# The first norm of a two-layer encoder: a scaled input turned by transposes, in place of a product with a diagonal

## The chip, the core and the metric

The kernel runs on one core of one Trainium2 chip. The metric is the time of one execution on the device, in microseconds; lower is better. The engines are TensorE (PE, with its weight loads as PEld), VectorE (DVE), ScalarE (ACT), GpSimd (POOL) and SyncE (SP), which here only issues loads and stores.

## What is computed

Two layers of a streaming encoder on 256 tokens of 1024 channels, in float32. Cut to what matters here:

```python
for l in range(DEPTH):                       # DEPTH = 2
    h = rmsnorm(x, pre_norm_g[l])            # x * rsqrt(mean(x*x) + EPS) * g, along the channels
    proj = h @ w_in[l]                       # 1024 -> 10432
    (u, v, z_a, c_q, c_kv, k_rope, z_b, x_c, z_c, g_a, g_b, g_c) = split(proj)
    y_a = gmlp_spatial(u, v, ...) * silu(z_a)
    y_b = mla_attention(c_q, c_kv, k_rope, ...) * silu(z_b)
    y_c = rg_lru(x_c, ...) * silu(z_c)
    merged = sigmoid(g_a) * (y_a @ w_proj_a[l]) + sigmoid(g_b) * (y_b @ w_proj_b[l]) + sigmoid(g_c) * (y_c @ w_proj_c[l])
    x = x + rmsnorm(merged @ w_out[l], post_norm_g[l])
```

The change touches how the first layer's `h` is made, and what stands around it.

## The kernel before, in words

The 256 tokens are two tiles of 128 (`NT = 2`), the 1024 channels eight tiles of 128 (`KT = 8`). The weights are streamed in chunks, 1 MB for most of them. A chunk is loaded by SyncE's queue into one of three raw buffers (`load`, L186), and is then split into two tiles of the type float32r: a high part (ScalarE, L242) and the remainder (VectorE, L243). A product is three passes of TensorE: high by high, high by low, low by high (L280 to L283, L407 to L409, L521 to L523). Three pairs of split tiles exist (`pairs`); `done` gives one back and `pump` splits the next chunk into it, and then asks for further loads, of which each waits until its raw buffer has been split.

The order of the work on each engine is the order in which the program writes it (`tc.manual_schedule()`, L432); nothing is reordered. A wait therefore holds all that was written behind it on the same engine, and a load that waits holds SyncE's queue.

The head of the program (L433 to L503) goes as follows. GpSimd writes `ones`, `mhalf` and the identity. ScalarE's queue loads the eight rows of `pre_norm_g` (`g8`). SyncE's queue loads token tile 0 in two halves (L439), the first half of chunk 0, token tile 1 (L440), the second half of chunk 0, chunks 1 and 2, four tables of the rotary embedding (L443 to L446) and nine small rows of constants (`layer_consts`, L297 to L307), which TensorE turns later in one transpose (L319) before the last of the eight rank steps.

Fourteen products of `ones` (`warm`, L453) fill TensorE while the input arrives. For a token tile, `first_norm` (L457) squares one half on ScalarE and the other on VectorE and makes the factor `rstd` (a sum on VectorE, L372, a power on GpSimd, L373). `diagonal` (L465) puts the factor on a diagonal, and `first_turn` (L470) multiplies the eight channel tiles by it (L473), which scales and transposes in one product; the result is evicted tile by tile, 128 columns each, by ScalarE with the gain as its scale (`hT[0]`, L477), and by VectorE, which leaves the remainder (`hT[1]`, L479). The gain as a column, `g0`, comes from a transpose of `g8` (L488, L489). `second_norm` (L492) runs between the two halves of the split of chunk 0: it makes tile 1's factor and then evicts tile 0. `second_turn` (L501) turns tile 1; it is called from within the first rank step, behind its first two rows of tiles, and it also splits chunks 1 and 2.

The rank steps (`ranks`, L513) multiply the four first chunks, each of 4 x 128 rows and 384 or 320 columns: chunk 0 by tiles 0 and 1, chunk 1 by both, and so on; chunks 0 and 2 need the channel tiles 0 to 3 of `hT`, chunks 1 and 3 the tiles 4 to 7. After them comes the first of the wide products (`recur_in`, L658, through L281 to L283).

The second layer's norm is made otherwise: `pre_norm` (L380) squares on ScalarE, scales 512 columns at a time on VectorE with the gain as a row (L388), and `pre_transpose` (L391) turns them by transposes (L396) and evicts 512 columns at a time (L399, L400).

Of the kernel before, what the change touches and what calls it, by code (L numbers as in the profile page):

```python
# [13 lines left out]
P = 128  # L14
# [3 lines left out]
NT = 2  # L18
# [67 lines left out]
def tile_trunk(ctx: ExitStack, tc, I, out):  # L86
# [99 lines left out]
    def load(c, parts=1, mid=None):  # L186
        n = c.kt * c.cols
        c.raw = raw_()
        if c.lru is None:
            raw, src, m = v2(c.raw[:, :n], c.cols), c.src(), c.kt // parts  # L190
            for i in range(parts):
                nc.sync.dma_start(raw[:, i * m : (i + 1) * m], src[:, i * m : (i + 1) * m])
                if i == 0 and mid:
                    mid()
            return
# [101 lines left out]
    def layer_consts(l, rows):  # L297
        G.memset(rows[64:R_N], 0.0)
        for name, r0, n in (
# [3 lines left out]
            nc.sync.dma_start(rows[r0 : r0 + n], I[name][l].rearrange("(t p) -> t p", p=P))  # L303
        nc.sync.dma_start(rows[R_CW : R_CW + 40], I["lru_conv_w"][l].rearrange("w (t p) -> (w t) p", p=P))
        for name, r0 in (("lru_b_a", R_BA), ("lru_b_x", R_BX)):
            nc.sync.dma_start(rows[r0 : r0 + NB, :BW], I[name][l].rearrange("(b p) -> b p", p=BW))
# [125 lines left out]
    with tc.manual_schedule():  # L432
# [7 lines left out]
        load(chunks[0], parts=2, mid=lambda: nc.sync.dma_start(X[:, 1], I["x"][0, P : 2 * P, :]))  # L440
        state["dma"] = 1
        loads_to(2)
        nc.sync.dma_start(cosT, I["cosT"])  # L443
        nc.sync.dma_start(sinT, I["sinT"])
        nc.sync.dma_start(cosK, I["cosK"].rearrange("(t p) f -> p t f", p=P))
        nc.sync.dma_start(sinK, I["sinK"].rearrange("(t p) f -> p t f", p=P))  # L446

        lc = layer_consts(0, slot("rows", (P,)))


        def warm(n):
            for _ in range(n):
                mm(aux()[:, :P], ones, ones, start=True, stop=True)  # L453

        g0 = small("g0", KT)

        def first_norm(t):  # L457

            ss = sums(2)
            mean_square(X[:, t, :512], ss[:, 0:1])  # L460
            x = X[:, t, 512:]
            V.scalar_tensor_tensor(tmp(), x, 1.0 / D, x, ALU.mult, ALU.mult, accum_out=ss[:, 1:2])
            return rsqrt_sum(ss)

        def diagonal(r):  # L465
            d = tmp()[:, :P]
            V.tensor_scalar(d, ident, r, None, ALU.mult)
            return d

        def first_turn(t, d, take, mid=None):  # L470
            ps = [take(), take()]
            for k in range(KT):
                mm(ps[k // 4][:, k % 4 * P : (k % 4 + 1) * P], X[:, t, k * P : (k + 1) * P], d, start=True, stop=True)  # L473
            for b in range(2):
                todo = [(b * 4 + k, ps[b][:, k * P : (k + 1) * P]) for k in range(4)]
                for k, o in todo:
                    act(hT[0][:, t, k], o, AF.Copy, scale=g0[:, k : k + 1])  # L477
                for k, o in todo:
                    V.scalar_tensor_tensor(  # L479
                        hT[1][:, t, k], o, g0[:, k : k + 1], f(hT[0][:, t, k]), ALU.mult, ALU.subtract  # L480
                    )
                if b == 0 and mid:
                    mid()

        warm(14)
        d0 = diagonal(first_norm(0))
        ps = aux()
        nc.tensor.transpose(ps[:, :KT], g8, ident[:KT, :KT])  # L488
        V.tensor_copy(g0, ps[:, :KT])  # L489
        ds = []  # L490

        def second_norm():  # L492
            r = first_norm(1)
            first_turn(0, d0, bank, lambda: ds.append(diagonal(r)))
            warm(1)

        split(chunks[0], parts=2, mid=second_norm)
        state["split"] = 1
        loads_to(3)

        def second_turn():  # L501
            first_turn(1, ds[0], aux, lambda: pump(1, parts=2))
            pump(parts=2)  # L503

        for l in range(L):
# [53 lines left out]
            for i in range(8):  # L559
                j, t = (i // NT, i % NT) if l == 0 else (i % 4, i // 4)  # L560
                if i == 7:
                    layer_consts2(lc)
                ranks(j, t, turns.get((j, t)))
# [533 lines left out]
```

## Time and profile before

| | |
|---|---|
| time of the runs shown, three | 788.27, 788.53, 789.82 us; median 788.53 |
| the profiled execution, its own time | 790.08 us |
| its span, from the first to the last instruction | 788.3 us |
| mean granted TensorE clock over the span | 0.997 |
| loaded and stored by DMA | 163.43 MB, 207 GB/s on average |

The page gives each engine's busy time, the span in 40 slices, the DMA queues, the chain of work that ended last, and the costliest groups of instructions. Of one instruction the timeline gives the start from the start of the span and the length, both in us, then the engine, the line, the operation and the tiles, `out<-in`, and in brackets how long its engine stood idle ahead of it and who released it. A line of the windows has the busy time of PE, PEld, DVE, ACT and POOL in one stretch, the number of instructions behind each, the clock that was granted to TensorE (1.00 is full speed), the busy share of the DMA engines, and what they moved in GB/s. A product of two plain float32 tiles shows as two records in the count of a row.

### The profile page before, as it was taken

Reading aid. Unit: us, or ns where it says so; the run is one execution under the profiler, and the core shown is the slowest. Engines: PE = TensorE matmul, PEld = TensorE weight load, DVE = VectorE, ACT = ScalarE, POOL = GpSimd, SP = SyncE. Lnnn points to the kernel's source line nnn. Section 1 sums busy time; section 2 is a strip of 40 time slices with the busy share of each in tenths; the row PEclk is TensorE's granted clock in tenths of the full one; section 3 lists DMA queues with packets and bytes.
Section 4 is the critical chain, followed back from the end, with each engine's and each line's share of the span. In section 5 each row is a group of like instructions: output and inputs, shape, how many; then the busy total and the mean of one; then the engine's idle time right before and its main releaser. Section 6 shows DMA issues by size and latency. Waiting matters only on the chain.

```text
span 788.3 us, 15228 instructions
## 1 busy us (share of the span) xinstructions
PE 778.4 (99%) x6381; PEld 771.4 (98%) x6381; DVE 540.4 (69%) x708; ACT 472.3 (60%) x705; POOL 39.2 (5%) x78
## 2 busy tenths in 40 slices
PE   8999999999999999999999999999999999999996
PEld 8999999999999999999999999999999999999996
DVE  5587776676569579556666887767665776885562
ACT  5687675446595585433556868544657856744441
POOL 1100420000000000000010006000000000000000
PEclk9999999999999999999999999999999999999999
DMA  7845657469989767556357555764799869566521
GB/s 226 284 151 190 210 178 212 130 169 305 295 235 293 244 195 262 187 187 215 114 173 241 167 181 167 241 162 130 215 315 289 255 223 317 181 219 213 180 88 54
DMA packets 162669, 163.43 MB, mean 207 GB/s; under 512 B 16510, under 2 KB 159272, under 8 KB 162600
## 3 DMA queue, kind: packets, MB, share of 16 engines
q1 hardware_dynamic: 162584, 162.45, 66.5%
q8 instruction: 50, 0.82, 0.4%
q14 instruction: 19, 0.16, 0.0%
q10 hardware_dynamic: 16, 0.00, 0.0%
HBM read 150.91 MB, written 11.53 MB: 206 GB/s over the span
## 4 chain that ended last, share of the span: by engine, by line
PE 96%; issue 2%; DMA 1%; ACT 1%; DVE 0%; SPq 0%; POOLq 0%; POOL 0%; DVEq 0%; ACTq 0%
PE mm L281 24%; PE mm L282 24%; PE mm L283 24%; PE mm L409 2%; PE mm L407 2%; PE mm L408 2%; PE mm L715 1%; PE mm L523 1%; PE mm L521 1%; PE mm L522 1%; PE aux L829 1%; PE aux L756 1%; DMA X<-in_x_dram 1%; PE mm L907 1%; PE mm L906 1%
## 5 line engine op out<-in xcount | busy, mean ns | idle before, releaser
L243 DVE TENSOR_TENSOR wlo<-raw,whi 128x2048 fp32r<-128x2048 f32 (+5 forms) x123 | 263.9, 2149 | 135.1 <-ACT whi L242 134.8
L281 PE MATMUL mm<-hT,whi 128*128 128x256 f32 x1088 | 306.8, 282 | 0.0
L283 PE MATMUL mm<-hT,wlo 128*128 128x256 f32 x1088 | 304.9, 280 | 0.0
L282 PE MATMUL mm<-hT,whi 128*128 128x256 f32 x1088 | 304.9, 280 | 0.0
L242 ACT ACTIVATE whi<-raw 128x2048 fp32r<-128x2048 f32 (+5 forms) x123 | 221.0, 1802 | 90.4 <-PE mm L282 71.2
L282 PEld LDWEIGHTS mm<-hT,whi 128*128 128x128 f32 x1088 | 204.9, 188 | 0.5 <-issue 0.5
L281 PEld LDWEIGHTS mm<-hT,whi 128*128 128x128 f32 x1088 | 204.9, 188 | 0.5 <-issue 0.5
L283 PEld LDWEIGHTS mm<-hT,wlo 128*128 128x128 f32 x1088 | 204.8, 188 | 0.0
L281 PE MATMUL mm<-ya,whi 128*128 128x256 f32 x128 | 36.1, 282 | 1.0 <-ACT t L861 1.0
L407 PE MATMUL mm<-whi,hT 128*128 128x256 f32 x128 | 36.5, 285 | 0.0
L409 PE MATMUL mm<-whi,hT 128*128 128x256 f32 x128 | 36.1, 282 | 0.0
L282 PE MATMUL mm<-ya,whi 128*128 128x256 f32 x128 | 36.0, 281 | 0.0
L283 PE MATMUL mm<-ya,wlo 128*128 128x256 f32 x128 | 36.0, 281 | 0.0
L281 PE MATMUL mm<-yc,whi 128*128 128x256 f32 x128 | 36.0, 281 | 0.0
L408 PE MATMUL mm<-wlo,hT 128*128 128x256 f32 x128 | 36.0, 281 | 0.0
L281 PE MATMUL mm<-yb,whi 128*128 128x256 f32 x128 | 35.9, 281 | 0.0
L283 PE MATMUL mm<-yb,wlo 128*128 128x256 f32 x128 | 35.9, 281 | 0.0
L282 PE MATMUL mm<-yc,whi 128*128 128x256 f32 x128 | 35.9, 281 | 0.0
L283 PE MATMUL mm<-yc,wlo 128*128 128x256 f32 x128 | 35.9, 280 | 0.0
L282 PE MATMUL mm<-yb,whi 128*128 128x256 f32 x128 | 35.9, 280 | 0.0
L373 POOL TENSOR_TENSOR rstd<-rstd,mhalf 128x1 f32<-128x1 f32 x8 | 4.4, 549 | 547.7 <-DVE rstd L372 547.7
L428 ACT ACTIVATE mg<-acc 128x512 fp32r<-128x512 f32 x8 | 5.1, 632 | 42.8 <-DVE acc L881 42.8
(253 smaller groups left out, 1601.8 us busy)
## 6 DMA issues: line engine op xcount, KB each, us to landing
raw<-in_w_in_dram SPq DMA_DIRECT2D x76, 1024.0 KB
raw<-in_w_proj_a_dram SPq DMA_DIRECT2D x8, 1024.0 KB
raw<-in_w_proj_b_dram SPq DMA_DIRECT2D x8, 1024.0 KB
raw<-in_w_proj_c_dram SPq DMA_DIRECT2D x8, 1024.0 KB
raw<-in_w_out_dram SPq DMA_DIRECT2D x8, 1024.0 KB
xs<-xh SPq DMA_DIRECT2D x16, 320.0 KB
raw<-in_mla_w_uq_dram SPq DMA_DIRECT2D x8, 576.0 KB
raw<-in_mla_w_ukv_dram SPq DMA_DIRECT2D x4, 1024.0 KB
```

The lines of the kernel that those rows point to most:

```text
L242: act(hi[:, w], c.raw[:, w], AF.Copy)
L243: V.tensor_tensor(lo[:, w], c.raw[:, w], f(hi[:, w]), ALU.subtract)
L281: mm(ps, lh, rh, start=start, stop=False)
L282: mm(ps, lh, rl, start=False, stop=False)
L283: mm(ps, ll, rh, start=False, stop=stop)
L407: mm(ps, lh, rh, start=k == 0, stop=False)
L408: mm(ps, lh, rl, start=False, stop=False)
L409: mm(ps, ll, rh, start=False, stop=k == KT - 1)
L521: mm(ps, lh, rh, start=j % 2 + k == 0, stop=False)
L522: mm(ps, lh, rl, start=False, stop=False)
L523: mm(ps, ll, rh, start=False, stop=j % 2 * 4 + k == KT - 1)
L715: mm(o, qn[:, ts], kn[:, :n], start=True, stop=False)
```

## The change

- Token tile 1 is loaded right behind tile 0, ahead of chunk 0, and chunk 0 comes in four parts of one row of tiles each, not in two. The two cosine and sine tables for the queries (`cosT`, `sinT`) are loaded later, behind the splits of chunks 1 and 2; the two for the key stay where they were.
- The nine loads of constants of the first layer go through GpSimd's queue, and are written behind the two factors. In the second layer they stay with SyncE.
- Eight products of a column of the identity with `g8` lay the gain out as a row on all partitions, in two PSUM tiles `gb` of 512 columns (`gains_bcast`), between six and four warming products; the transpose of `g8` and its copy go.
- Both halves of both token tiles are squared by ScalarE, ahead of all its other work.
- VectorE scales the input by the factor and the gain, 512 columns at a time, into `h`; TensorE turns `h` by transposes, four per bank; ScalarE evicts 512 columns in one instruction, and VectorE leaves the remainder of 512 columns in one. The diagonals go.
- Chunk 0 is split by rows of tiles (384 columns), and VectorE's order is written out: first remainder of tile 0, first split, scaling of tile 1's first half, three splits, then the two second halves.
- The turn is in three pieces: tile 0's channel tiles 0 to 3 ahead of the rank steps, tile 1's within the first of them (`second_turn`), and the tiles 4 to 7 of both ahead of the second rank step (`third_turn`), with the splits of chunk 1 in four parts around the last eviction.

The diff, cut to its core:

```diff
@@ load
-                if i == 0 and mid:
+                if i == parts // 2 - 1 and mid:
...
-    def layer_consts(l, rows):
+    def layer_consts(l, rows, q=nc.sync):
...
-            nc.sync.dma_start(rows[r0 : r0 + n], I[name][l].rearrange("(t p) -> t p", p=P))
+            q.dma_start(rows[r0 : r0 + n], I[name][l].rearrange("(t p) -> t p", p=P))
...
-        load(chunks[0], parts=2, mid=lambda: nc.sync.dma_start(X[:, 1], I["x"][0, P : 2 * P, :]))
+        nc.sync.dma_start(X[:, 1], I["x"][0, P : 2 * P, :])
+        load(chunks[0], parts=4)
         state["dma"] = 1
         loads_to(2)
-        nc.sync.dma_start(cosT, I["cosT"])
-        nc.sync.dma_start(sinT, I["sinT"])
...
-        lc = layer_consts(0, slot("rows", (P,)))
...
+        gb = [aux(), aux()]
+        def gains_bcast():
+            for k in range(KT):
+                mm(gb[k // 4][:, k % 4 * P : (k % 4 + 1) * P], ident[:KT, k : k + 1].to_broadcast([KT, P]), g8,
+                   start=True, stop=True)
+        def first_sums(t):
             ss = sums(2)
...
+                mean_square(X[:, t, b * 512 : (b + 1) * 512], ss[:, b : b + 1])
+            return ss
+        def first_scale(t, h, r, b):
+            cs = slice(b * 512, (b + 1) * 512)
+            V.scalar_tensor_tensor(h[:, cs], X[:, t, cs], r, gb[b], ALU.mult, ALU.mult)
+        def first_turn(t, h, b, take):
+            ps = take()
+            for k in range(4):
+                c0 = (b * 4 + k) * P
+                nc.tensor.transpose(ps[:, k * P : (k + 1) * P], h[:, c0 : c0 + P], ident)
+            return v2(ps, P)
+        def first_hi(t, b, ps):
+            act(hT[0][:, t, b * 4 : b * 4 + 4], ps, AF.Copy)
+        def first_lo(t, b, ps):
+            V.tensor_tensor(hT[1][:, t, b * 4 : b * 4 + 4], ps, f(hT[0][:, t, b * 4 : b * 4 + 4]), ALU.subtract)
...
-        warm(14)
-        d0 = diagonal(first_norm(0))
...
-        split(chunks[0], parts=2, mid=second_norm)
+        warm(6)
+        gains_bcast()
+        warm(4)
+        h = [slot("h", (D,)) for _ in range(NT)]
+        ss = [first_sums(t) for t in range(NT)]
...
+        r0 = rsqrt_sum(ss[0])
+        first_scale(0, h[0], r0, 0)
+        ps = first_turn(0, h[0], 0, bank)
+        first_hi(0, 0, ps)
+        r1 = rsqrt_sum(ss[1])
+        first_lo(0, 0, ps)
+        split_hi(c, 0, 4)
+        split_lo(c, 0, 1)
+        first_scale(1, h[1], r1, 0)
+        split_lo(c, 1, 4)
+        first_scale(0, h[0], r0, 1)
+        first_scale(1, h[1], r1, 1)
         state["split"] = 1
         loads_to(3)
+        lc = layer_consts(0, slot("rows", (P,)), G)
         def second_turn():
-            first_turn(1, ds[0], aux, lambda: pump(1, parts=2))
+            t10 = first_turn(1, h[1], 0, aux)
+            first_hi(1, 0, t10)
+            first_lo(1, 0, t10)
+        def third_turn():
+            t01, t11 = (first_turn(t, h[t], 1, aux) for t in (0, 1))
+            first_hi(0, 1, t01)
+            first_lo(0, 1, t01)
+            def rest():
+                first_hi(1, 1, t11)
+                first_lo(1, 1, t11)
+            pump(1, parts=4, mid=rest)
             pump(parts=2)
+            nc.sync.dma_start(cosT, I["cosT"])
+            nc.sync.dma_start(sinT, I["sinT"])
...
+                if l == 0 and i == 1:
+                    third_turn()
                 ranks(j, t, turns.get((j, t)))
```

More of the change, by code (lines that the diff above doesn't have):

```diff
@@ L302, in layer_consts @@
         ):
-            nc.sync.dma_start(rows[r0 : r0 + n], I[name][l].rearrange("(t p) -> t p", p=P))
-        nc.sync.dma_start(rows[R_CW : R_CW + 40], I["lru_conv_w"][l].rearrange("w (t p) -> (w t) p", p=P))
+            q.dma_start(rows[r0 : r0 + n], I[name][l].rearrange("(t p) -> t p", p=P))
+        q.dma_start(rows[R_CW : R_CW + 40], I["lru_conv_w"][l].rearrange("w (t p) -> (w t) p", p=P))
         for name, r0 in (("lru_b_a", R_BA), ("lru_b_x", R_BX)):
-            nc.sync.dma_start(rows[r0 : r0 + NB, :BW], I[name][l].rearrange("(b p) -> b p", p=BW))
+            q.dma_start(rows[r0 : r0 + NB, :BW], I[name][l].rearrange("(b p) -> b p", p=BW))
         return {"rows": rows}
@@ L446, in tile_trunk @@
         nc.sync.dma_start(sinK, I["sinK"].rearrange("(t p) f -> p t f", p=P))
-        lc = layer_consts(0, slot("rows", (P,)))
         def warm(n):
             for _ in range(n):
-                mm(aux()[:, :P], ones, ones, start=True, stop=True)
-        g0 = small("g0", KT)
-        def first_norm(t):
-            ss = sums(2)
[L460 to L473, printed above, removed]
-            for b in range(2):
[L475 to L483, printed above, removed]
@@ L485, in tile_trunk @@
-        warm(14)
-        d0 = diagonal(first_norm(0))
[L487 to L495, printed above, removed]
-        split(chunks[0], parts=2, mid=second_norm)
+                mm(bank()[:, :P], ones, ones, start=True, stop=True)
+        gb = [aux(), aux()]
[3 more added lines that the diff above has]
+                   start=True, stop=True)
@@ new lines, in first_hi, with split_hi, split_lo @@
+        def first_hi(t, b, ps):
+            act(hT[0][:, t, b * 4 : b * 4 + 4], ps, AF.Copy)
+        def first_lo(t, b, ps):
+            V.tensor_tensor(hT[1][:, t, b * 4 : b * 4 + 4], ps, f(hT[0][:, t, b * 4 : b * 4 + 4]), ALU.subtract)
+        def split_hi(c, k0, k1):
+            for k in range(k0, k1):
+                w = slice(k * c.cols, (k + 1) * c.cols)
+                act(c.pair[0][:, w], c.raw[:, w], AF.Copy)
+        def split_lo(c, k0, k1):
+            for k in range(k0, k1):
+                w = slice(k * c.cols, (k + 1) * c.cols)
+                V.tensor_tensor(c.pair[1][:, w], c.raw[:, w], f(c.pair[0][:, w]), ALU.subtract)
@@ new lines, in tile_trunk @@
+        warm(6)
[3 more added lines that the diff above has]
+        ss = [first_sums(t) for t in range(NT)]
+        c = chunks[0]
+        c.pair = pairs.pop(0)
+        c.hi, c.lo = (v2(x[:, : c.kt * c.cols], c.cols) for x in c.pair)
+        r0 = rsqrt_sum(ss[0])
[5 more added lines that the diff above has]
+        split_hi(c, 0, 4)
```

## The prediction

> **What bounds the kernel now.** I read the page first, then the waits of TensorE, then the windows, the chain of waits and the timeline of the head. The page:
>
> ```profile
> PE 778.4 (99%) x6381; PEld 771.4 (98%) x6381; DVE 540.4 (69%) x708; ACT 472.3 (60%) x705; POOL 39.2 (5%) x78
> PE 96%; issue 2%; DMA 1%; ACT 1%; DVE 0%; SPq 0%; POOLq 0%; POOL 0%; DVEq 0%; ACTq 0%
> ```
>
> TensorE is busy for 99% of the span and carries 96% of the chain that ended last. Its waits from 16 us to the end are one line:
>
> ```profile
> PE mm L281 <- ACT t L861: 1.0, 2, 0.5
> ```
>
> So the kernel is a head, in which TensorE is not full, and then a stream that nothing interrupts. A change in the head is worth what it moves the start of that stream, less the work that it leaves to be done in the stream. The windows of the head (busy us of PE, PEld, DVE, ACT, POOL, then the granted clock, the DMA share and GB/s):
>
> ```profile
> 2.00:4.00 2.00, 2.00 (x11) 2.00 (x11) 0.00 (x0) 1.16 (x3) 0.00 (x0) 1.00 0.77 284
> 4.00:6.00 2.00, 2.00 (x16) 1.90 (x15) 1.08 (x4) 0.18 (x2) 0.60 (x2) 1.00 0.84 185
> 6.00:8.00 2.00, 2.00 (x18) 1.96 (x18) 0.23 (x2) 0.67 (x1) 0.00 (x0) 1.00 0.96 353
> 8.00:10.00 2.00, 0.83 (x7) 0.56 (x5) 1.66 (x4) 1.58 (x7) 0.00 (x0) 1.00 1.06 397
> 10.00:12.00 2.00, 1.46 (x7) 0.90 (x6) 1.69 (x8) 2.00 (x7) 0.55 (x1) 0.86 1.07 395
> 12.00:14.00 2.00, 2.00 (x10) 2.00 (x11) 1.59 (x4) 0.24 (x2) 0.00 (x0) 0.50 0.73 216
> 14.00:16.00 2.00, 2.00 (x14) 2.00 (x13) 0.96 (x4) 2.00 (x6) 0.00 (x0) 0.79 0.08 20
> ```
>
> TensorE is idle for 1.7 us between 8 and 12, and the granted clock then falls to 0.50 for 12 to 14, with parts of the neighbouring windows: 0.86 is 0.56 us of half clock (0.14 x 2 / 0.5), 0.79 another 0.84 us, so some 3.4 us from about 11.45 to 14.85. The chain of waits (start, length) and the timeline around it:
>
> ```profile
> 2.11 6.46 DMA X<-in_x_dram
> 9.32 1.03 ACT hT L477 x4
> 10.38 0.36 DVE hT L479
> 11.89 3.38 PE aux L473 x16
> ```
> ```profile
> 0.97 5.12 PE L453 MATMUL aux<-ones 128*128 128x128 f32 x28 [0.97 <-POOL ones L433]
> 6.18 2.05 PE L473 MATMUL mm<-t,X 128*128 128x128 f32 x16
> 9.62 0.45 PE L521 MATMUL mm<-whi,hT 128*128 128x384 f32 x1 [1.17 <-ACT hT L477]
> 10.78 0.45 PE L523 MATMUL mm<-whi,hT 128*128 128x384 f32 x1 [0.54 <-DVE hT L479]
> 15.03 0.42 PE L521 MATMUL mm<-whi,hT 128*128 128x384 f32 x1
> 22.53 0.31 PE L521 MATMUL mm<-whi,hT 128*128 128x320 f32 x1
> ```
>
> The second token tile lands at 8.57 and ScalarE squares it before it evicts the first one. The same eight matmuls of a turn take 2.05 us for token tile 0 and 3.38 us for tile 1, at half clock. From 15.03 the stream runs. Of the 96 rank matmuls (4 chunks, 2 tiles, 4 rows of tiles, 3 products) six are done by then, so 90 are left. From 15.03 to 22.53 there are 42 of them: 0.18 us each.
>
> **The change, part by part.** After it, twelve rank matmuls and eight transposes stand ahead of the last eight transposes, and the stream starts behind those with 84 rank matmuls left. Against 15.03 with 90 that is a credit of 6 x 0.18 = 1.07 us. What remains is when the last transpose ends. The durations:
>
> ```profile
> 405.01 1.42 DVE L388 SCALAR_TENSOR_TENSOR h<-X,rstd,pre_norm_g 128x512 f32<-128x512 f32 x2 [0.66 <-POOL rstd L373]
> 405.92 1.22 PE L396 MATMUL aux<-ident,h 128*128 128x128 f32 x8
> 406.89 0.39 PE L521 MATMUL mm<-whs,hT 128*128 128x320 f32 x1
> 407.18 1.31 DVE L400 TENSOR_TENSOR hT<-aux,hT 128x512 fp32r<-128x512 f32 x2 [0.76 <-ACT hT L399]
> ```
> ```profile
> L399 ACT ACTIVATE hT<-aux x2: 597/598/599, 406.5 to 407.2; 128x512 fp32r<-128x512 f32 x2
> ```
> ```profile
> 0.72 0.86 SPq L439 DMA_DIRECT2D X<-in_x_dram  x2
> 3.46 0.63 ACT L378 ACTIVATE t<-X 128x512 f32<-128x512 f32 x1 [0.84 <-DMA X<-in_x_dram]
> 3.99 0.19 ACT L378 ACTIVATION_READ_ACCUMULATOR t<-X 128x1 f32 x1
> 4.11 0.69 DVE L462 SCALAR_TENSOR_TENSOR t<-X 128x512 f32<-128x512 f32 x1 [4.11 <-DMA X<-in_x_dram]
> 4.94 0.16 DVE L372 TENSOR_REDUCE rstd<-ssq 128x1 f32<-128x3 f32 x1
> 5.77 0.29 DVE L467 TENSOR_SCALAR t<-ident,rstd 128x128 f32<-128x128 f32 x1 [0.67 <-POOL ssq L367]
> 7.33 0.84 ACT L242 ACTIVATE whi<-raw 128x768 fp32r<-128x768 f32 x1 [3.15 <-DMA raw<-in_w_in_dram]
> 8.21 0.96 DVE L243 TENSOR_TENSOR wlo<-raw,whi 128x768 fp32r<-128x768 f32 x1 [1.76 <-ACT whi L242]
> 19.80 1.28 ACT L242 ACTIVATE whi<-raw 128x1280 fp32r<-128x1280 f32 x1 [1.04 <-DMA raw<-in_w_in_dram]
> 21.11 1.49 DVE L243 TENSOR_TENSOR wlo<-raw,whi 128x1280 fp32r<-128x1280 f32 x1 [0.70 <-ACT whi L242]
> ```
>
> The second layer's norm already has the new form, so its rows price it: a scaling of 512 columns 0.71 us, a transpose 0.12 (0.97 for eight), a high eviction 0.60, a low one 0.66 and VectorE follows it 0.68 behind (407.18 against 406.5). Eight transposes take 0.97 us where eight matmuls took 2.05: 1.1 us of TensorE per tile, or 2.2 in all at full clock. A split of 384 columns isn't in the trace: half of 768 gives 0.48 on VectorE, the slope from 768 to 1280 gives 0.56; I take 0.52. On ScalarE it is 0.42 to 0.51, and I take 0.45.
>
> *Second tile first.* Its landing is bounded by 5.4 (the first tile at 4.11 and 524 kB at 397 GB/s) and by today's 8.57. With the rates of the windows, 185 until 6 and 353 after it, it is 1.89 x 185 = 350 kB and 0.5 us more: 6.5, which I take. The quarters of chunk 0 then have 1.25 MB ahead of or in the first: 0.94 by 6 (284 and 185 GB/s for 2 us each), the rest at 353: about 7, and one each 0.55 behind, all ahead of their splits below.
>
> *ScalarE* now squares both halves of both tiles ahead of all else. Behind tile 1's squares, which wait for its landing, are queued the first high eviction and the four high splits, and VectorE's subtractions and the first rank matmul wait for those. Two squares and the reading of the sum take 0.53 + 0.63 + 0.19 = 1.35: 6.5 to 7.85. First high eviction 7.85, high splits from 8.45.
>
> *TensorE's* warm-up grows from 14 to 18 products at 0.26 (2.05 / 8): to about 7.1, four transposes to 7.6. The squares hide this; if tile 1 came at 5.4 it would be the bound, at 7.7 instead of 7.85.
>
> *VectorE* carries the path. Low eviction at 8.53, then in its order: 0.66, split 0.52, scaling of tile 1 0.71, three splits 1.56, two scalings 1.42. The marks: 9.2, 9.7, 10.4, 12.0, 13.4. Tile 1's factor (0.83 us from the reduction's start to its first use) is ready at 8.7, under the low eviction.
>
> *At full clock* the last four transposes run from 13.55 to 14.05, and the stream begins there: 0.98 early, and 1.07 of credit. *At half clock from 11.45*, as now: transposes of tile 1 from 11.45 at 0.24, to 12.4; the six rank matmuls at 0.36, to 14.55; one more transpose before 14.85; the other seven to 15.7. TensorE itself is then the bound, and the landing of tile 1 matters less. A half-clock stretch that starts at 10 costs less, as some of it falls on TensorE's waits: about 15.0.
>
> The idle that brings the stretch on is larger than now: between 7.6 and 11.45 TensorE has the first three products and two of the next, 1 us of work at most in nearly 4. So I take the half clock as staying.
>
> *At nothing:* the cosine tables go behind waits for two raw buffers; their first use is far behind:
>
> ```profile
> 50.77 0.42 DVE L621 TENSOR_TENSOR t<-mm,cosT 128x256 f32<-128x256 f32 x1
> ```
>
> Nine small loads leave SyncE's queue, so chunk 3 is asked for when the last split of chunk 0 ends (12.0). The next product's split has slack:
>
> ```profile
> 25.67 2.29 DVE L243 TENSOR_TENSOR wlo<-raw,whi 128x2048 fp32r<-128x2048 f32 x1 [3.07 <-ACT whi L242]
> 29.69 0.28 PE L281 MATMUL mm<-hT,whi 128*128 128x256 f32 x1
> ```
>
> It ends at 27.96 and is wanted at 29.69; a stream one microsecond early still finds it. If that cover were gone, each microsecond more would be lost there.
>
> **Sum.** The profiled execution took 790.08 with a span of 788.3. With the half clock: + (15.7 - 15.03) - 1.07 = -0.4 when the stretch lies as it does now, -1.1 when it starts at 10; 789.3 is the middle. The runs shown are 788.27, 788.53 and 789.82, so the profiled one is 1.55 above their median. The stretch costs 1.33 us in the second turn, nearly that difference; that the median's run was free of it is likely and not shown. So the change removes some 1 us of the profiled execution, but makes certain a stretch that the median run may have been spared. Against the median, 789.3 is 0.1% more, under the 0.2% (1.6 us) that a measurement of this kernel can tell from no change.
>
> **Rivals.**
>
> *The clock stays full* (28%). Then 790.08 - 0.98 - 1.07 = 788.0; at the favourable ends (tile 1 at 5.4, cheap splits) 787.4. Against it: 1.17 and 0.54 us of idle brought it on in this trace. The Trainium skill ("TensorE: Matmul & The Clock Gate", Why this matters for your kernels) asks only that no gap passes about 3 us; by that the clock would stay full and the time would be 788.0. The trace disagrees, since 1.7 us of idle in four were enough.
>
> *The second tile comes late and holds ScalarE* (12%): slower. The window from 4 to 6 moves only 185 GB/s, and if that is the price of first touching each input, tile 1 pays it too. At 8.57 all of VectorE's marks go back by 2.05: rank matmuls wait, at half clock until 14.85, for splits that end at 14.05, and the last transposes end at 16.8: 790.08 + 1.77 - 1.07 = 790.8. It decides from a landing of about 7.7 on.
>
> *A second half-clock stretch* (6%). If transposes didn't count as work for the clock, 14.85 to 18.25 would also run at half speed: 1.7 us, 791.0. Six rank matmuls fill 2.1 of the 3.4 us of the stretch, more than the share at which the clock now fell, so I think it unlikely. The Trainium skill (the same page, Part 4) says that PE transposes don't count as PE-busy in the same way, which speaks against this change; no row here shows it, the second layer's eight being surrounded by matmuls.
>
> *Pool's queue is slow* (4%). Nine loads start behind tile 1's factor at about 9.0; the transpose of their rows is due here:
>
> ```profile
> L319 PE MATMUL aux<-ident,rows x1: 261/261/261, 27.8 to 27.8; 113*128 113x113 f32 x1
> ```
>
> With 2.74 us to land (0.72 to 3.46), that leaves about 16 us, or 1.7 each. SyncE takes 0.43 for an issue; I take 1 on Pool, whose other work waits behind them (the ranks' factors, after 27.8). At 2.2 each it is 4 us late: 793. The Trainium skill ("DMA: Bandwidth & Descriptors", Latency and other measured facts) gives about 1 us to the first byte on that path against 0.6; no row here shows it.
>
> **How the numbers follow.** Forecast 46%, of which 4 lie above 790.1 (a late tile in part); clock full 28%, of which 5 lie below 786.95; 12, 6 and 4% as above; 4% for a gain that no row shows. Slower 0.26, faster 0.09, same 0.65. 787.4 to 791.0 leaves out some 8% on each side.
>
> **What would show it.** The granted clock near 0.5 for about 3.4 us from 10 to 15; tile 1's square starting near 6.5; VectorE's last scaling ending near 13.4; the last transposes ending between 15 and 15.7; transposes at 0.12 us (0.24 at half clock). Wrong it is if a square of tile 1 starts after 7.7, if ranks wait at the rows' transpose, or if the stream begins before 13.

## The result, and the profile after

| | before | after |
|---|---|---|
| median of the runs (range) | 788.8 us (788.27 to 789.82, 4 runs) | 793.45 us (793.13 to 793.75, 4 runs) |
| ratio, 95% interval | | 1.0057, 1.004 to 1.0075 |
| profiled execution: time, span | 790.08, 788.3 us | 793.13, 791.4 us |

The change makes the kernel 0.57% slower, 4.7 us; the forecast was 789.3 with 791.0 as its upper end. The two profiled executions are 3.1 us apart. Executions of one and the same kernel lie 2 to 3 us apart, so medians are compared with medians and a profile with its own time. The other 1.6 us between the medians come from which executions were profiled: that of before lies 1.3 us above its median, that of after 0.3 below. Before's has a stretch at half clock (11.45 to 14.86) that none of the seven profiles of kernels made from before, further down, has after its first full clock.

The page of the kernel after, the two lines that answer to those of before:

```profile
PE 781.7 (99%) x6370; PEld 774.1 (98%) x6370; DVE 539.7 (68%) x697; ACT 471.7 (60%) x701; POOL 44.3 (6%) x87
PE 97%; issue 2%; ACT 0%; DVE 0%; POOL 0%; POOLq 0%; DVEq 0%; ACTq 0%
```

About as many TensorE instructions, and 3.3 us more of busy time: TensorE was not kept waiting, it worked more slowly. The timeline of TensorE in the head (start, length, then what):

```profile
0.98 2.93 PE L450 MATMUL mm<-ones 128*128 128x128 f32 x12 [0.98 <-POOL ones L433]
3.84 3.78 PE L457 MATMUL aux<-t,ident 8*128 8x128 f32 x16
7.54 2.08 PE L450 MATMUL mm<-ones 128*128 128x128 f32 x8
9.41 1.06 PE L474 MATMUL mm<-ident,h 128*128 128x128 f32 x4
11.57 0.69 PE L552 MATMUL mm<-whi,hT 128*128 128x384 f32 x1 [1.10 <-ACT whi L486]
16.74 1.04 PE L474 MATMUL aux<-ident,h 128*128 128x128 f32 x8
17.53 0.42 PE L552 MATMUL mm<-whi,hT 128*128 128x384 f32 x1
31.13 0.28 PE L281 MATMUL mm<-hT,whi 128*128 128x256 f32 x1
```

The eight gains' products (16 records) last 3.78 us, 0.47 each, where the prediction counted 0.26; the warming products behind them, 0.52. The uninterrupted stream starts at 17.53, against 15.03, and the first wide product at 31.13, against 29.69. The transposes by the source view (min/median/max ns, first and last start):

```profile
L474 PE MATMUL aux<-ident,h x12: 272/273/421, 14.3 to 17.5; 128*128 128x128 f32 x12
L474 PE MATMUL mm<-ident,h x4: 420/421/422, 9.4 to 10.1; 128*128 128x128 f32 x4
```

The same instruction takes 421 ns at 9.4 and 272 at the end: half clock until some 16 us (the first full clock in the clock record, the list of changes of the granted clock, is at 16.34). ScalarE and VectorE over the same stretch:

```profile
7.11 0.63 ACT L378 ACTIVATE t<-X 128x512 f32<-128x512 f32 x1 [2.24 <-DMA X<-in_x_dram]
8.25 0.19 ACT L378 ACTIVATION_READ_ACCUMULATOR t<-X 128x1 f32 x1
10.51 0.60 ACT L478 ACTIVATE hT<-mm 128x512 fp32r<-128x512 f32 x1 [2.07 <-PE mm L474]
```
```profile
11.14 0.69 DVE L481 TENSOR_TENSOR hT<-mm,hT 128x512 fp32r<-128x512 f32 x1 [2.51 <-ACT hT L478]
14.28 1.40 DVE L468 SCALAR_TENSOR_TENSOR h<-X,rstd,aux 128x512 f32<-128x512 f32 x2
```

ScalarE had tile 1's squares behind it at 8.4 and then stood 2.07 us for TensorE's transposes. The head gives 31.13 - 29.69 = 1.44 us. The rest of the 3.1 lies where nothing was changed; the last two products of before and of after:

```profile
781.67 0.28 PE L1004 MATMUL aux<-wls,mg 128*128 128x256 f32 x1
781.79 0.28 PE L1005 MATMUL aux<-whs,mg 128*128 128x256 f32 x1
```
```profile
784.80 0.28 PE L1037 MATMUL aux<-wls,mg 128*128 128x256 f32 x1
784.92 0.27 PE L1038 MATMUL aux<-whs,mg 128*128 128x256 f32 x1
```

From the first wide product to the last one it is 752.10 us before and 753.79 after: 1.69 us more. Two stretches in it by the windows (length, PE busy and instructions, clock, DMA share, GB/s), before and after:

```profile
284.00:330.00 46.00, 46.00 (x390) 1.00 0.61 196
645.00:715.00 70.00, 70.00 (x599) 1.00 0.70 225
```
```profile
284.00:330.00 46.00, 46.00 (x394) 1.00 0.63 204
645.00:715.00 70.00, 70.00 (x592) 1.00 0.70 224
```

TensorE is busy throughout at full clock in both, and in the longer one seven products fewer get done after the change: 0.1182 us each against 0.1169. The shorter one goes the other way, with four products more. So two things are to be explained, 1.4 us of head and 1.7 us of stream.

### The profile page after: what moved, and what is told of

It is laid out like the page before. It is cut to its first block, busy times and chain, and to the rows that moved or that the text cites. A ratio compares the mean times of both kernels' runs of the same rounds, so it can differ in the third digit from the quotient of the medians.

```text
span 791.4 us, 15210 instructions
## 1 busy us (share of the span) xinstructions
PE 781.7 (99%) x6370; PEld 774.1 (98%) x6370; DVE 539.7 (68%) x697; ACT 471.7 (60%) x701; POOL 44.3 (6%) x87
## 4 chain that ended last, share of the span: by engine, by line
PE 97%; issue 2%; ACT 0%; DVE 0%; POOL 0%; POOLq 0%; DVEq 0%; ACTq 0%
PE mm L281 24%; PE mm L282 24%; PE mm L283 24%; PE mm L409 2%; PE mm L407 2%; PE mm L408 2%; PE mm L553 1%; PE mm L748 1%; PE mm L554 1%; PE mm L552 1%; PE aux L862 1%; PE aux L789 1%; PE mm L939 1%; PE mm L940 1%; PE aux L1037 1%
```

## The experiments

In this section "head" is the start of the first wide product, and "stream" the time from there to the last product. Every kernel was timed against before on its own chip.

### The clock in the head

**The kernel after once more.**

> The changed kernel as it is, timed again beside the kernel before on the same chip. Theory (TensorE stays at half clock to about 16 us, whatever the phase of the clock's windows): 3 to 5 us above before, and the first rise to full clock again after 12 us, the four transposes of tile 0 again at 0.26 us each. Rival (an unlucky phase of free-running windows): in a new execution the rise comes near 5 us and the time falls to 1 us from before. Second rival (the stream itself runs slower by some tenths of a per cent in what was taken with the changed kernel, not because of it): less than 2.5 us above before.

793.32 us (6 runs), ratio 1.005 (1.0036 to 1.0063); head 30.91, span 791.2. The loss is there again.

**The gains' products contract 128 rows, of which 120 are zero, instead of 8.**

```diff
-        g8 = tmp()[:KT, :P]
+        g8 = tmp()[:, :P]
+        V.memset(g8, 0.0)
...
-                mm(gb[k // 4][...], ident[:KT, k : k + 1].to_broadcast([KT, P]), g8, ...)
+                mm(gb[k // 4][...], ident[:, k : k + 1].to_broadcast([P, P]), g8, ...)
```

> The changed kernel with the gains' products contracting 128 rows, of which 120 are zero: same number of products, same order, same results. Theory (an 8-row product does not count as work for the clock, by the rows it uses): the clock rises by 5 us, the transposes of tile 0 end near 7.6, the first high eviction starts at about 8.5, and the time falls by 1 to 2.5 us against the changed kernel. If what counts is how much data is not zero, or the place of the products, nothing changes and the rise stays at about 16.

791.43 us, ratio 1.0027 (1.0016 to 1.0039); head 28.09. Its timeline of TensorE and the source view of the transposes:

```profile
3.70 3.48 PE L458 MATMUL aux<-t,ident 128*128 128x128 f32 x16
7.01 1.06 PE L451 MATMUL mm<-ones 128*128 128x128 f32 x8
```
```profile
L475 PE MATMUL mm<-ident,h x4: 272/272/273, 7.9 to 8.2; 128*128 128x128 f32 x4
```

The warming products behind the gains take 1.06 us instead of 2.08, and the transposes 272 ns from the first one on. The number of products and the bytes out are the same: only the rows contracted differ. On this chip 1.9 us of the loss is this (793.32 to 791.43). The same work timed on another chip (a_128_slots16, below, whose unused buffers moved nothing) has a ratio of 1.0013, by which it would be 2.9 (an estimate from the two ratios). In the profiles the head falls by 2.8 to 3.0.

**All 14 warming products, and ahead of the gains.**

```diff
-        warm(6)
+        warm(14)
         gains_bcast()
-        warm(4)
```

> The changed kernel with all fourteen products of ones ahead of the gains, none behind. Theory (full products bring the full clock, the products that contract only 8 rows do not): the clock rises near 4.6 us as before the change, the gains take 2.1 us and not 3.8, the first high eviction starts near 9.2 and not at 10.5, and the time falls by 1 to 2.5 us against the changed kernel. Rival (the number of products or the transposes decide, not their kind): the clock stays down to about 16 us, and with four more products ahead of the first transpose the time is 0.5 to 1 us longer.

792.73 us, ratio 1.0049 (1.0037 to 1.0061): 0.6 less than after, where 1 to 2.5 were expected. The full clock is reached before the gains (they take 2.04 us there) but goes again. Its windows (busy time of PE, PEld, DVE, ACT, POOL, clock, DMA share, GB/s):

```profile
10.00:12.00 2.00, 0.98 (x2) 0.58 (x3) 1.50 (x3) 2.00 (x5) 2.00 (x5) 0.59 0.98 319
12.00:14.00 2.00, 2.00 (x7) 1.60 (x7) 2.00 (x5) 0.12 (x1) 2.00 (x5) 0.50 0.10 23
14.00:16.00 2.00, 2.00 (x9) 2.00 (x8) 1.67 (x3) 0.60 (x1) 0.80 (x2) 0.50 0.57 106
```

The clock record has half clock from 10.35 to 17.18: two stretches of 3.41 us in a row, after one in which TensorE had little but 8-row products. The place of the warming products alone does not mend it.

**The kernel before, its warming products contracting 8 rows.**

```diff
-                mm(aux()[:, :P], ones, ones, start=True, stop=True)
+                mm(aux()[:, :P], ones[:KT], ones[:KT], start=True, stop=True)
```

> The kernel before with its fourteen warming products contracting 8 rows in place of 128 (their result is used by nothing). Theory: the clock no longer rises near 4.6 us, the turn of tile 0 runs at half speed (4 us in place of 2.05), and the time is 2 to 4 us above before. Rival (rows don't matter to the clock): as before within 0.5 us.

789.53 us, ratio 1.0011 (1.0002 to 1.0021). In the timeline the 28 records take 6.34 us where before took 5.12:

```profile
0.97 6.34 PE L453 MATMUL aux<-ones 8*128 8x128 f32 x28 [0.97 <-POOL ones L433]
```

The clock record has its first full clock at 10.15, against 4.62 in before and 4.54 to 6.69 in all seven profiles with before's warming products. The reverse test agrees: TensorE is as busy as before, and the clock does not come. The time was expected to rise by 2 to 4 us and rose by 0.4. That is a miss; in this profile TensorE still ran without a wait from 11.01 on and had no stretch at half clock later.

### The stream

In the kernels after, whole products of 48 run at another pace than in before, always the same: 120.0 ns a matmul near 240 us where before has 117.4, 117.3 near 300 where it has 118.6, 118.65 near 670 where it has 117.35. A reason to try comes from the compiled programs and not from a profile: `h` holds two of the 16 large working buffers while the next are handed out, and eight of the 16 change places for the rest of the program. The first kernels built to test this did not move those addresses.

**Two buffers taken and not used, in before.**

```diff
+        for _ in range(2):
+            slot("pad", (P,))
         lc = layer_consts(0, slot("rows", (P,)))
```

> The kernel before with two slot buffers taken and not used ahead of the constants' rows, so that every later slot buffer lies two places on, as after the change; nothing else differs. Theory (the place of the operands in SBUF sets the pace of the products in stretches): from the first wide product to the last, 753.8 us as in all four profiles of the changed kernel's family, not 752.1, and the time 1.5 to 1.9 us above before. Rival (the pace comes from the rings of PSUM banks or of small buffers, or from the chip): 752.1 and the time of before.

789.16 us, ratio 1.0 (0.9992 to 1.0009); before's paces (600 products in 645 to 715). Inconclusive: a buffer that nothing uses is given back at once, so no other one moved, and counted from 30 us on every product keeps its time in before to some 0.01 us. The waits of TensorE show something else:

```profile
PE mm L283 <- DVE wlo L243: 1.3, 1, 1.3
```

With no half-clock stretch in this profile TensorE comes to the first wide product at 28.10 and waits 1.3 us for its split.

**Before, with its scratch ring and its second ring of banks moved on** by six and two, as in after.

```diff
+        for _ in range(6):
+            tmp()
+        for _ in range(2):
+            aux()
         g8 = tmp()[:KT, :P]
```

> The kernel before with the ring of 512-column buffers advanced by six and that of the auxiliary PSUM banks by two, as they stand after the change; slots as before. Theory of the slots: 752.1 us from the first wide product to the last, no change of the time. Rival: 753.8 and 1.7 us more.

790.01 us, ratio 1.0004 (0.9996 to 1.0013), before's paces (599 products). These two rings are not the cause.

**The 128-row gains and 14 unused buffers, and the same with five products behind the first turn.** In the second one the fifth product overwrites the bank of tile 0's first turn, so a part of `h` is replaced.

```diff
         h = [slot("h", (D,)) for _ in range(NT)]
+        for _ in range(14):
+            slot("pad", (P,))
...
         ps = first_turn(0, h[0], 0, bank)
+        warm(5)
```

> The changed kernel with the gains' products over 128 rows, and fourteen more slot buffers taken and not used, so that with the two of the scaled input the slots are sixteen on, which is none. Theory of the slots: 752.1 us from the first wide product to the last where the same kernel without the fourteen has 754.0, first wide product again at 28.1, and a time of 788.4 to 789.6, the kernel before within 0.1%. Rival (rings or chip): 754.0 again and 791.4.

> The same with five more warming products behind the first turn, where TensorE waits for the first split. Theory (a spell of half clock comes in part of the executions after the idle between the turn and the first rank products): the spread of the times shrinks, the slow ones above by 1 to 2 us are gone, and the median is 0.3 to 0.8 us under the kernel without them; the first wide product stays at 28.1. If the spells come for another reason, nothing changes.

790.18 us, ratio 1.0013 (1.0004 to 1.0021), and 791.47, ratio 1.003 (1.0021 to 1.004); the kernel after's paces in both (593 products in the first). Again no other buffer moved, and neither expected gain came. The half clock came in both profiles, in the second from 11.21 to 14.62: five products there do not keep it away.

**Before, with two buffers really held** (one column of each cleared at both ends), so that all others lie at after's addresses; nothing else of the change.

```diff
+        held = [slot("h", (D,)) for _ in range(2)]
+        for x in held:
+            G.memset(x[:, :1], 0.0)
         lc = layer_consts(0, slot("rows", (P,)))
...
+                if l == 0 and i == 1:
+                    for x in reversed(held):
+                        G.memset(x[:, :1], 0.0)
```

> The kernel before, in which two of the 16 large working buffers are held from before the constants' rows until the second rank product, as h is held in the kernel after (Pool clears one column of each at both places). From then on every working buffer lies at the address that it has in the kernel after; nothing else of the change is in it. Theory (the 1.7 us that the kernel after loses between its first wide product and its last product come from where the working buffers lie): that stretch takes 753.8 us instead of 752.1, whole products of 48 run at the other kernel's paces (117.4 ns a matmul where before has 118.6 near 300 us, 120.0 where it has 117.4 near 240 us), and the time is 788.9 + 1.7 = 790.6, a ratio near 1.002. Rival (it comes from the banks of the sums, from the small tiles, or from something else that the new norm shifts): 752.1 us, before's paces, a ratio of 1.000.

790.45 us, ratio 1.0026 (1.0017 to 1.0035). The same windows of this kernel:

```profile
284.00:330.00 46.00, 46.00 (x394) 1.00 0.63 198
645.00:715.00 70.00, 70.00 (x592) 1.00 0.69 223
```

394 and 592 products, as in after. Counted from 30 us on, each product against the same one of before, this kernel has lost 1.23 us by the last of them, after 1.69. Its median lies 1.95 us above before's, which holds more than the stream: ahead of 30 us its profile has a wait of 0.7 us for a split.

**The kernel after with 128-row gains, and `h` in four scratch buffers**, so that the working buffers lie as in before.

```diff
-        h = [slot("h", (D,)) for _ in range(NT)]
+        h = [[tmp() for _ in range(2)] for _ in range(NT)]
...
-            V.scalar_tensor_tensor(h[:, cs], X[:, t, cs], r, gb[b], ALU.mult, ALU.mult)
+            V.scalar_tensor_tensor(h[b], X[:, t, cs], r, gb[b], ALU.mult, ALU.mult)
```

> The kernel after with the gains' products contracting 128 rows (as measured before at 791.4) and with the scaled input h in four 512-column scratch buffers instead of two of the large working buffers, so that every later working buffer lies where it lies in the kernel before. Theory (placement): the stretch from the first wide product to the last product is 752.1 us again, and the time 791.4 - 1.7 = 789.7, a ratio near 1.001. Rival (banks of the sums, small tiles or something else): 753.8 us, 791.4, a ratio near 1.003.

788.36 us, ratio 1.0001 (0.9992 to 1.001): the loss is gone. Windows, and waits from 30 us on:

```profile
284.00:330.00 46.00, 46.00 (x390) 1.00 0.61 195
645.00:715.00 70.00, 70.00 (x600) 1.00 0.70 225
```
```profile
PE mm L281 <- ACT t L894: 1.0, 2, 0.5
```

These are before's paces: counted from 30 us on, every product keeps its time in before to some 0.01 us. The waits, near 195 and 580, are at 1.0 in sum again; they were 1.3 in after. (Ahead of 30 us TensorE waits 0.5 us for the split of the first wide chunk.) So the addresses cost the stream 1.2 us by themselves, and the 0.4 to 0.5 more that after loses near 580 us goes with them too, though addresses alone don't bring it about. Which access meets which is not shown; the profiles hold no addresses. The median is 3.1 us under the 791.43 of the kernel with 128-row gains alone, where 1.7 were expected. The two were timed on different chips, and profile against profile it is 1.5 us (790.29 and 788.76).

### The other parts of the change, and what the head is worth

**ScalarE's squares of tile 1 behind the first eviction and two splits** (in the kernel just shown).

```diff
-        ss = [first_sums(t) for t in range(NT)]
+        ss = [first_sums(0)]
...
-        r1 = rsqrt_sum(ss[1])
         first_lo(0, 0, ps)
-        split_hi(c, 0, 4)
+        split_hi(c, 0, 2)
         split_lo(c, 0, 1)
+        ss.append(first_sums(1))
+        r1 = rsqrt_sum(ss[1])
+        split_hi(c, 2, 4)
+        split_lo(c, 1, 2)
         first_scale(1, h[1], r1, 0)
-        split_lo(c, 1, 4)
+        split_lo(c, 2, 4)
```

> The same kernel, and ScalarE's squares of tile 1 stand behind the first high eviction and the first two high splits instead of ahead of them. Theory (ScalarE held at tile 1's landing, the second rival of the prediction, is what bounds the head once the clock is full): the first high eviction starts at 7.0 to 7.5 instead of 8.8, the first wide product 0.5 to 1 us earlier than in the kernel without the new order, and the time is 0.5 to 1 us below it: 788.7 to 789.2. Rival (the scaling of tile 1 only comes later by as much as the first split comes earlier): the first wide product within 0.2 us, the time the same.

790.7 us, ratio 1.002 (1.001 to 1.003): a miss, 2.3 us slower. TensorE's waits in its timeline:

```profile
9.11 0.44 PE L555 MATMUL mm<-whi,hT 128*128 128x384 f32 x1 [1.10 <-ACT whi L486]
11.46 0.44 PE L556 MATMUL mm<-wlo,hT 128*128 128x384 f32 x1 [0.78 <-DVE wlo L491]
12.66 1.12 PE L474 MATMUL aux<-ident,t 128*128 128x128 f32 x4 [0.58 <-DVE t L469]
```

The first product comes 0.27 earlier, but tile 1's factor and its scaling come 1.8 later (11.86 instead of 10.02), TensorE waits at each step, and the clock halves from 12.67. The change's order was the better one.

**Before, with the new order of the loads alone** (tile 1 ahead of chunk 0).

```diff
-        load(chunks[0], parts=2, mid=lambda: nc.sync.dma_start(X[:, 1], I["x"][0, P : 2 * P, :]))
+        nc.sync.dma_start(X[:, 1], I["x"][0, P : 2 * P, :])
+        load(chunks[0], parts=2)
```

> The kernel before with one part of the change alone: token tile 1 is loaded ahead of the first weight chunk instead of between its halves. Theory (the order of the loads costs little by itself): the first half of the chunk lands some 1.3 us later (512 KB at near 400 GB/s), the first rank products start some 1 us later, tile 1's norm earlier; the time is 788.9 to 789.9, a ratio of 1.000 to 1.001. Rival (the order of the loads carries a good part of the loss in the head): a ratio of 1.002 or more.

790.72 us, ratio 1.0022 (1.0011 to 1.0034): the rival. ScalarE's first split waits for its data until 8.41, where before has 7.33:

```profile
8.41 0.84 ACT L242 ACTIVATE whi<-raw 128x768 fp32r<-128x768 f32 x1 [4.26 <-DMA raw<-in_w_in_dram]
```

**The kernel with 128-row gains and `h` in scratch, with before's order of the loads.**

```diff
-        nc.sync.dma_start(X[:, 1], I["x"][0, P : 2 * P, :])
-        load(chunks[0], parts=4)
+        load(chunks[0], parts=4, mid=lambda: nc.sync.dma_start(X[:, 1], I["x"][0, P : 2 * P, :]))
```

> The kernel with the 128-row gains and h in scratch buffers (788.4), with tile 1 loaded between the halves of the first weight chunk as in the kernel before. Theory (the new order of the loads is right for the new order of the work, since ScalarE squares tile 1 ahead of everything else): tile 1 lands some 1 us later, the first high eviction starts 0.8 to 1.2 us later, and the time is 789.0 to 789.8. Rival (the first weight chunk's landing is what counts here as it is in the kernel before, where the new load order alone cost 1.7 us): 788.0 or less.

791.2 us, ratio 1.0019 (1.0009 to 1.0028). Each order of the work has its own order of the loads, and the other one costs some 0.2% in both.

**Before, with the constants on Pool's queue alone.**

```diff
-        lc = layer_consts(0, slot("rows", (P,)))
...
         split(chunks[0], parts=2, mid=second_norm)
         state["split"] = 1
         loads_to(3)
+        lc = layer_consts(0, slot("rows", (P,)), G)
```

> The kernel before with one part of the change alone: the nine loads of the constants go through Pool's queue, issued after the first split, instead of SP's. Theory (this part costs and gains nothing): nine issues of 0.5 us on Pool from near 11 to 16 us, the rows land long before their transpose at 25, SP comes to its weight loads 3 us earlier, the time is within 0.3 us of before, a ratio of 0.9995 to 1.0005. Rival (the earlier weight loads give the first wide chunk's split time, and with it up to 1 us): 788 or less, a ratio under 0.9995.

788.61 us, ratio 0.9996 (0.9987 to 1.0004). No difference.

**Three steps on from the kernel with 128-row gains and `h` in scratch**: the first wide chunks split in halves; then also half of tile 1's square on VectorE and the warming products ahead of the gains; then also seven products of `ones` into a spare bank where TensorE idles.

```diff
-                        done(c)
+                        done(c, parts=2 - l)
```
```diff
+                V.scalar_tensor_tensor(tmp(), x, 1.0 / D, x, ALU.mult, ALU.mult, accum_out=ss[:, 1:2])
...
-        warm(6)
+        warm(10)
         gains_bcast()
-        warm(4)
```
```diff
         ps = first_turn(0, h[0], 0, bank)
+        fill(5)
...
                     mm(ps, lh, rh, start=j % 2 + k == 0, stop=False)
+                    if l + j + t == 0 and k < 2:
+                        fill(1)
```

> The kernel with the 128-row gains and h in scratch buffers (788.4), and in the first layer the chunks that are split when a rank chunk is done are split in two halves, so that the first wide product can start on the first half. Theory (with the clock and the placement put right, the head's gain is cut off by the split of the first wide chunk: its data land at 24.3, the high split takes 1.9 and the low split 2.3, and TensorE waits 0.5 for it at 28.6): the first wide product starts near 28.0 and no wait of over 0.2 us for a low split is left before 35; the time is 0.5 to 0.8 us lower, 787.6 to 787.9. Rival (TensorE, not the split, sets the end of this stretch): the same time, 788.4, the wait gone without effect.

> The same, and all ten warm-up products ahead of the gains' products, and the second half of tile 1's square on VectorE, as the kernel before has it. Theory (the first high eviction now waits for ScalarE's two squares of tile 1, 1.24 us, though its transposes are done): it starts at 7.8 instead of 8.34, the stream of rank products 0.5 us earlier, the first wide product near 27.2 to 27.5, and the time is 0.4 to 0.6 us below the kernel without these two edits: 787.0 to 787.4. Rival (TensorE idle for longer ahead of the first rank product falls back to half clock in most executions): 789 or more, with a half-rate stretch of 3.4 us between 10 and 16.

> The kernel of the run before that has the 128-row gains, h in scratch buffers, the first wide chunks split in halves and half of tile 1's square on VectorE (788.7; in its twelve executions 787.8 to 788.2 or 789.2 to 789.4), with seven products of the warm-up's kind in the idle time of TensorE ahead of the stream, into a bank that nothing reads: five behind the first four transposes, one behind each of the first two high products. Theory (the two groups of times are executions without and with a stretch at half clock ahead of the stream, and idle time of TensorE brings it): fewer of the slower group, a median of 787.9 to 788.2, a ratio under 0.999, and no half-rate stretch between 10 and 16 us in the profile. Rival (such a stretch comes with other causes, or the idle time left is still enough): both groups as before, 788.7 or more.

789.75, 788.69 and 788.31 us; ratios 1.0002 (0.9992 to 1.0013), 0.9993 (0.9985 to 1.0002), 0.9994 (0.9985 to 1.0003). A window of the second and of the third:

```profile
12.00:14.00 2.00, 2.00 (x9) 2.00 (x8) 1.69 (x3) 0.60 (x1) 1.70 (x4) 0.50 0.70 135
```
```profile
12.00:14.00 2.00, 1.86 (x14) 1.54 (x13) 1.22 (x3) 0.74 (x3) 1.33 (x3) 1.00 0.83 187
```

All three medians lie above what was expected of them. The first two were profiled with a half-clock stretch (789.96 and 789.17), the third without one and without any wait of TensorE from 2 to 60 us: head 27.05, span 785.6, 787.41. Its eleven executions lie within 787.41 to 788.85, those of the second in two groups, 787.78 to 788.21 and 789.17 to 789.44. No version beats before by more than can be measured.

What brings the stretch on can be read from the 20 profiles together. Two changes in one clock record always lie a whole number of 3.41 us apart, and these steps lie elsewhere in each execution. One step of before and one of b_tmp_aux, both at full clock:

```profile
8.03:11.44 3.41, 1.71 (x10) 1.00 1.06 397
```
```profile
7.95:11.37 3.42, 1.99 (x11) 1.00 1.06 392
```

TensorE is busy for 50% of the first, and half clock follows; it is busy for 58% of the second, and the clock stays full. In the first 30 us of all 20 profiles half clock followed seven steps that were busy for 42 to 53%, and an eighth (a_warm14_first) that was busy for 85% with its 8-row products and for 27% without them. The steps after which the clock stayed full were busy for 58% or more, but for one at 53% (a_htmp_loads). The longest single gap does not decide: 1.29 us in a_128_htmp brought no stretch, 1.10 us in a_best_all did. So idle time brings the stretch on by its share of a step, and where the steps happen to lie decides whether an execution has it. That would make two groups of times out of one kernel; only one execution of each was profiled.

**Before, with the constants on Pool's queue and the first wide chunks in halves** (both edits as above).

> The kernel before with two parts alone: the constants' loads on Pool's queue (788.6 by itself), and the chunks that are split when a rank chunk is done split in halves. Theory (in executions without a stretch at half clock the kernel before, too, waits 1.3 us for the split of its first wide chunk, and halves take most of that): those executions 0.8 to 1.2 us faster, the median near 788.0, a ratio of 0.9985 to 0.9995. Rival (nothing ahead of the first wide product reaches the end but the clock): a ratio of 0.9995 to 1.0005.

788.32 us, ratio 0.9996 (0.9987 to 1.0005): the rival. The wait for the split is not in its profile, but the gain doesn't show either.

## Why the prediction was wrong, step by step

- **TensorE's warm-up "grows from 14 to 18 products at 0.26 (2.05 / 8): to about 7.1, four transposes to 7.6".** This step failed. The price was taken from products at full clock; here they took 0.47 to 0.52, the transposes started at 9.41, and the first high eviction was at 10.51 instead of 7.85. It missed what kind of product the eight new ones are: with 8 rows they don't bring the full clock (a_gains_128rows, b_warm_8rows). "The squares hide this" fell with it.
- **The clock.** A half-clock stretch was forecast, 3.4 us from 11.45 as before, brought on by idle time. It was half clock from the start to 16.3: the direction was right, cause and length were not. The stream began at 17.53 and not at 15.7, so this term was +2.50 instead of +0.67. That the median execution of before is spared the stretch was called likely and not shown; the seven profiles of kernels made from before bear it out.
- **The credit** of 1.07 held: 29.69 - 15.03 = 14.66 us of rank products before, 31.13 - 17.53 = 13.60 after, 1.06.
- **"A change in the head is worth what it moves the start of that stream, less the work that it leaves to be done in the stream."** The second failed step: the pace of the stream was taken as untouched. The head's edit moved buffers that the rest of the program uses, and the stream took 1.69 us longer. Summed anew: 790.08 + 2.50 - 1.06 + 1.69 = 793.21, measured 793.13 (the profiled executions).
- **Tile 1** landed at 7.11, forecast 6.5, within the bounds. The rival that it holds ScalarE did not decide here, since TensorE was later still; in a_gains_128rows it did (tile 1 at 7.56, first high eviction at 8.80).
- **VectorE's durations** were right: 4.54 us from the low eviction to the last scaling (11.14 to 15.68), forecast 4.87.
- **The clock stays full**, 788.0: with clock and addresses put right 788.36 came, and its profile has full clock from 6.02 us to the last product. But 788.0 stood for 2 us less than the profiled execution of before, and against before's median on the same chip, 788.5, nothing was gained, so that the numbers meet is in part luck. The trace of before had shown half clock after 1.7 us of idle time, against the rule of the Trainium skill ("TensorE: Matmul & The Clock Gate", Why this matters for your kernels) that no gap should pass some 3 us. The runs agree with the trace: in a_best_all half clock came with no gap over 1.1 us.
- **The rival on transposes** was not separated from the rest: in a_gains_128rows the clock stays full through all sixteen. Its argument took the share at which the clock fell for the one at which it rises; after a step that was busy for 80% (a_warm14_first, 10.35 to 13.77) the clock stayed at half.
- **Pool's queue**: an issue took 0.5 us, not 1 or more, and the rows' transpose found its rows.
- **"A stream one microsecond early still finds it."** Not always. The split of the first wide chunk moves from one execution to the next, and in several profiles with a better head TensorE met it (1.3 us in b_slots2, 0.7 in b_perm, 0.5 in a_128_htmp); in others with as good a head it did not (a_gains_128rows, 28.09).

## What to carry to other kernels

Price a new instruction at the clock that will be granted at its place, and see that what fills TensorE ahead of the real work contracts as many rows as the real work: eight products with 8 rows each cost 2 to 3 us here. A buffer taken from a shared pool for a moment changes the addresses of everything that is handed out later; compare the addresses of the two programs, and try the new buffer elsewhere, before explaining a change of pace in code that was not touched. In a head that waits for its data, each order of the work can have its own order of loads, as both did here.

## What the runs showed of the hardware

- Products that contract 8 rows last as long as those with 128 (at full clock eight take 2.04 us in a_warm14_first and 2.05 in before) and don't bring TensorE's full clock: the first full clock is at 10.15 us with such warming, at 4.54 to 6.69 with 128 rows. The Trainium skill ("TensorE: Matmul & The Clock Gate", What's actually happening) has the clock set by how busy TensorE has lately been. By the profile it was busy without a gap through the 8-row products of b_warm_8rows, 6.34 us, and the clock did not rise.
- A stretch at half clock lasts 3.41 us or twice that (11.45 to 14.86, 10.35 to 17.18). It followed steps of 3.41 us in which TensorE was busy for 53% or less. From half clock the full clock came after steps that were busy for 85% or more and not after those of 80% or less; 8-row products are left out of these shares.
- The clock column of the windows reads 1.00 before the first change on record. In after this is a trap: 1.00 throughout, with instructions at half speed until 16.3. Only their durations show it:

```profile
8.00:10.00 2.00, 2.00 (x11) 2.00 (x11) 0.16 (x1) 0.44 (x2) 1.23 (x3) 1.00 1.04 382
```

- At full clock and without a wait, groups of 48 products of the same shape run at fixed paces, most often 117.3, 118.65 or 120.0 ns a product, the same in every kernel with the same addresses, and exchanged where working buffers are exchanged. The Trainium skill ("SBUF — State Buffer", SBUF: two separate sides) has it that TensorE never waits for others at the memory; the runs show that where buffers lie costs the stream 1.23 us here (b_perm), and not by which path.
- Issuing a load of 1 to 20 kB occupies Pool for 0.5 us, the first one for 0.76:

```profile
9.47 0.76 POOL L303 DMA_DIRECT2D rows<-in_mla_q_norm_g_dram  x1
10.23 0.51 POOL L303 DMA_DIRECT2D rows<-in_mla_kv_norm_g_dram  x1
```
